# Reworked beginning of a one-core hybrid encoder layer: order of the input, the first weights and the first products

## Chip, core and metric

The kernel runs on one core of one Trainium2 chip. The metric is the device time of one execution in microseconds, as the median of several runs. The core has five engines: PE (TensorE, matrix products), DVE (VectorE), ACT (ScalarE), POOL (GpSimd) and SP (SyncE), which here only issues DMAs. Each engine works through its own instructions in the order of the program and waits on semaphores for the others.

## The reference

One layer on 512 tokens of 1024 channels, in float32: an RMS norm, one input projection to 11272 columns, two token mixers (an mLSTM and a stick-breaking attention) on parts of these columns, two projections back, gates, and an output projection with a residual.

```python
def reference(x, norm_w, w_in, b_in, conv_w, ...):
    h = rmsnorm(x, norm_w)                    # x * rsqrt(mean(x*x) + EPS) * norm_w
    proj = einsum('bsd,de->bse', h, w_in) + b_in
    (mq, mk, mv, mi, mf, mo, mz, sq, sk, sv, sz, gates) = split(proj, ...)
    ...                                       # mLSTM -> y_m, stick-breaking attention of
    ...                                       # rmsnorm(sq), rmsnorm(sk), sv -> y_s
    merged = g_m * (y_m @ w_proj_m) + g_s * (y_s @ w_proj_s)
    return x + merged @ w_out
```

The change touches only the norm and the first group of columns of the projection: the first 512 of `sq`, the queries of four attention heads.

## The kernel before

Every large product is made of three: each float32 operand is split into a high part (a rounded copy, type fp32r, made by ACT) and a low part (the operand less its high part), and high x high, low x high and high x low are summed in PSUM. The high and low parts of the normed, transposed input are called `hh` and `hl`, eight slices of 128 channels (index k) by 512 tokens; those of the first weights are `fh` and `fl`, eight tiles of 128x512 (index k), kept in the list `f_w`.

The work is a list of units, `units`, each with 512 KB of weights (`stg` is the tile that its DMA fills). In the loop over units, number c issues the evacuation of unit c - 1, the splits of units up to c + 2, then its own products in two halves, `mm(0)` and `mm(1)`, with other work (transposes, attention heads) put between the halves and behind them. The order that is written is the order on each engine. The first four units are special (`first=True` in `tok_group`): their weights are four pieces of 256 rows for the same 512 columns, and their products go by blocks of 128 tokens: unit tb computes block tb with all eight k, 24 products, into its own PSUM bank `f_ps[tb]`. From unit 4 on the general code runs (`mm3`, L85 to L87).

Before the loop stand the DMAs, all issued by SP in this order: the first token block of the input in two halves (`load_x(0)`, L193), the vector `norm_w` (8 rows of `v_rows`, L201), the weights of units 0 and 1 (L109), token block 1, the weights of units 2 and 3, token blocks 2 and 3, and a list of small vectors (`gst`, `load_vecs`). The bias row of the first group (`brow`, L297) and the weights of unit 4 follow from inside the loop.

Then PE gets nine products of a zero tile (`warm`, L910), the transposition of `norm_w` into `nw_t` (`norm_vec`), two further zero products, and the first token block's eight transposes. A token block is prepared in two steps. `x_scale(tb)` lets ACT square it and sum the squares (L271, L274), POOL form the reciprocal root (L260, L261) and DVE scale the block in place (L276). `x_turn(tb)` transposes it on PE in two groups of four (L286); DVE then makes `hh` of each group in one operation (L288) and `hl` in four (L292). The split of the first weights (`first_split`, L890 and L891) has ACT make `fh` and DVE (units 0 and 2) or POOL (units 1 and 3) make `fl`:

```python
    first_split(0)
    x_turn(0)
    first_split(1, nc.gpsimd)
    x_scale(1)
    first_split(2)
    first_split(3, nc.gpsimd)
```

The products of a block go k by k, three for each k (L932 to L934). Between the halves of unit 0 stands `x_turn(1)`, followed by `x_scale(2)`, `x_scale(3)` and POOL's `gates_fill`; between the halves of unit 1 stands `x_turn(2)`, behind them `x_turn(3)`. The evacuation of block 0 (in unit 1's turn, before its products) adds the bias row on DVE (`qraw`, L328) and takes four squares with sums on ACT (`sqj`, L337). Before unit 3's products PE transposes the small vectors (`turn_vecs`, L236 and L237).

Of the kernel before, what the change touches and what calls it, by code (L numbers as in the profile page):

```python
# [16 lines left out]
KT = 8  # L17
# [17 lines left out]
def tile_hybrid_layer(  # L35
# [58 lines left out]
    class Unit:  # L94
# [12 lines left out]
        def load(self, tag="stg"):  # L107
            self.st = blk(tag, shape=self.shape)
            nc.sync.dma_start(self.st, self.ap)  # L109
# [93 lines left out]
    rows(v_rows, 0, norm_w, 8)  # L203
# [59 lines left out]
    def x_scale(tb):  # L263
        xs = tiny.tile([128, 4], F32, name="xs", bufs=2)
        ssq, r = xs[:, 0:2], xs[:, 2:3]
        xn = x_t[tb]
        junk = blk("om", BF, (D,), name="junk")
        if tb == 0:
            for i in range(2):
                c = slice(i * D // 2, (i + 1) * D // 2)  # L270
                nc.scalar.activation(junk[:, c], xn[:, c], AF.Square, accum_out=ssq[:, i:i + 1])  # L271
            nc.gpsimd.tensor_tensor(ssq[:, 0:1], ssq[:, 0:1], ssq[:, 1:2], op=OP.add)
        else:
            nc.scalar.activation(junk, xn, AF.Square, accum_out=ssq[:, 0:1])  # L274
        rstd(r, ssq[:, 0:1], D, EPS)
        nc.vector.tensor_scalar(xn, xn, r, None, op0=OP.mult)  # L276

    def x_turn(tb):
        ts = slice(tb * 128, (tb + 1) * 128)
        xn = x_t[tb]  # L280
        for g in range(2):
            ks = slice(4 * g, 4 * g + 4)
            tp = att_ps()
            for j in range(4):
                kt = g * 4 + j
                nc.tensor.transpose(tp[:, j * 128:(j + 1) * 128], xn[:, kt * 128:(kt + 1) * 128], ident)  # L286
            dh = hh[:, ks, ts]
            nc.vector.tensor_tensor(dh, tp.rearrange("p (k t) -> p k t", k=4),  # L288
                                    nw_t[:, ks].unsqueeze(2).to_broadcast([128, 4, 128]), op=OP.mult)
            for j in range(4):  # L290
                k = 4 * g + j
                nc.vector.scalar_tensor_tensor(hl[:, k, ts], tp[:, j * 128:(j + 1) * 128], nw_t[:, k:k + 1],  # L292
                                               hh[:, k, ts].bitcast(F32), op0=OP.mult, op1=OP.subtract)
# [592 lines left out]
    def first_split(i, low=None):  # L886
        u = units[i]
        for j in range(2):
            hi, lo = blk("qk", FR, name="fh"), blk("y", FR, name="fl")
            nc.scalar.activation(hi, u.st[:, j, :], AF.Copy)  # L890
            (low or nc.vector).tensor_tensor(lo, u.st[:, j, :], hi.bitcast(F32), op=OP.subtract)  # L891
            f_w.append((hi, lo))

# [20 lines left out]
    x_scale(0)  # L914
    warm(2)
    first_split(0)
    x_turn(0)
    first_split(1, nc.gpsimd)
    x_scale(1)
    first_split(2)  # L920
    first_split(3, nc.gpsimd)

    f_ps = []

    def first_mm(tb):
        def mm(half):
            if half == 0:
# [117 lines left out]
```

## Time and profile before

| | |
|---|---|
| median of 3 runs | 719.08 us (718.85 to 719.39) |
| the profiled execution, its own time | 720.13 us |
| its span, first to last instruction | 718.4 us |
| mean granted clock of PE | 0.997 of full speed |
| PE busy | 709.8 us, 3356 products and transposes |
| DVE / ACT / POOL busy | 424.5 / 315.8 / 93.5 us |
| HBM read / written | 65.12 / 2.10 MB |

Times in the trace run from the start of the span. Lines are lines of the kernel; a name such as `dps<-fh,hh` is output and inputs. An entry "idle before" with an arrow is the idle time of the engine ahead of an instruction and what ended it. The end of a product on PE is modelled, since products are pipelined, so the distance between two starts says more than a duration.

### The profile page before, as it was taken

Reading aid. Unit: us, or ns where it says so; the run is one execution under the profiler, and the core shown is the slowest. Engines: PE = TensorE matmul, PEld = TensorE weight load, DVE = VectorE, ACT = ScalarE, POOL = GpSimd, SP = SyncE. Lnnn points to the kernel's source line nnn. Section 1 sums busy time; section 2 is a strip of 40 time slices with the busy share of each in tenths; the row PEclk is TensorE's granted clock in tenths of the full one; section 3 lists DMA queues with packets and bytes.
Section 4 is the critical chain, followed back from the end, with each engine's and each line's share of the span. In section 5 each row is a group of like instructions: output and inputs, shape, how many; then the busy total and the mean of one; then the engine's idle time right before and its main releaser. Section 6 shows DMA issues by size and latency. Waiting matters only on the chain.

```text
span 718.4 us, 9058 instructions
## 1 busy us (share of the span) xinstructions
PE 709.8 (99%) x3356; PEld 593.1 (83%) x3356; DVE 424.5 (59%) x663; ACT 315.8 (44%) x601; POOL 93.5 (13%) x235
## 2 busy tenths in 40 slices
PE   7999999999999999999999999999999999999997
PEld 5888888888888888888888888888888888888886
DVE  5837886656487568279944737994343254556441
ACT  5245364476255544244475534447554343222210
POOL 5422022253022112000001110000112000000000
PEclk9999999999999999999999999999999999999999
DMA  6433332233323222333332233333223333333621
GB/s 239 133 103 81 109 86 77 69 95 92 99 62 87 58 86 62 102 91 97 101 94 59 63 99 88 91 100 89 74 59 89 89 91 97 104 88 89 234 89 58
DMA packets 91475, 67.80 MB, mean 94 GB/s; under 512 B 3470, under 2 KB 77608, under 8 KB 91432
## 3 DMA queue, kind: packets, MB, share of 16 engines
q1 hardware_dynamic: 91432, 67.23, 32.8%
q8 instruction: 26, 0.43, 0.2%
q14 instruction: 17, 0.14, 0.1%
HBM read 65.12 MB, written 2.10 MB: 94 GB/s over the span
## 4 chain that ended last, share of the span: by engine, by line
PE 97%; DMA 1%; DVE 1%; POOL 0%; SPq 0%; issue 0%; ACT 0%; DVEq 0%
PE dps L85 28%; PE dps L87 27%; PE dps L86 27%; PE aps L86 2%; PE aps L87 2%; PE aps L85 2%; PE aps L440 1%; PE aps L382 1%; DMA stg<-in_w_in_dram 1%; PE dps L934 1%; PE dps L932 1%; PE dps L933 1%; PE aps L735 1%; PE aps L736 1%; PE aps L737 1%; DVE fl L891 0%
## 5 line engine op out<-in xcount | busy, mean ns | idle before, releaser
L91 DVE TENSOR_TENSOR wl<-stg,wh 128x1024 fp32r<-128x1024 f32 x108 | 132.3, 1225 | 140.3 <-ACT wh L90 139.9
L85 PE MATMUL dps<-hh,wh 128*128 128x512 f32 x448 | 175.8, 392 | 0.0
L86 PE MATMUL dps<-hl,wh 128*128 128x512 f32 x448 | 174.6, 390 | 0.0
L87 PE MATMUL dps<-hh,wl 128*128 128x512 f32 x448 | 174.6, 390 | 0.0
L90 ACT ACTIVATE wh<-stg 128x1024 fp32r<-128x1024 f32 x108 | 113.6, 1052 | 95.3 <-PE dps L87 58.6
L87 PEld LDWEIGHTS dps<-hh,wl 128*128 128x128 f32 x448 | 84.1, 188 | 17.7
L85 PEld LDWEIGHTS dps<-hh,wh 128*128 128x128 f32 x448 | 84.2, 188 | 17.5 <-issue 1.0
L86 PEld LDWEIGHTS dps<-hl,wh 128*128 128x128 f32 x448 | 84.2, 188 | 16.6
L85 PE MATMUL dps<-wh,hh 128*128 128x512 f32 x224 | 88.3, 394 | 0.0
L87 PE MATMUL dps<-wh,hl 128*128 128x512 f32 x224 | 87.4, 390 | 0.0
L86 PE MATMUL dps<-wl,hh 128*128 128x512 f32 x224 | 87.4, 390 | 0.0
L87 PEld LDWEIGHTS dps<-wh,hl 128*128 128x128 f32 x224 | 42.1, 188 | 8.9
L86 PEld LDWEIGHTS dps<-wl,hh 128*128 128x128 f32 x224 | 42.1, 188 | 8.2
L85 PEld LDWEIGHTS dps<-wh,hh 128*128 128x128 f32 x224 | 42.1, 188 | 8.2
L626 DVE SCALAR_TENSOR_TENSOR acc<-tmp,vec,acc 128x511 f32<-128x511 f32 (+2 forms) x48 | 36.0, 750 | 1.7
L629 ACT ACTIVATE tmp<-acc 128x512 f32<-128x512 f32 x16 | 10.1, 633 | 50.2 <-DVE acc L626 50.2
L415 DVE TENSOR_TENSOR_SCAN om<-om 128x512 f32<-128x512 f32 (+3 forms) x32 | 27.9, 871 | 6.3 <-POOL om L409 6.3
L409 POOL TENSOR_SCALAR_AFFINE_SELECT om<-om 128x128 f32<-128x128 f32 x32 | 12.1, 378 | 134.5 <-ACT om L407 134.5
L90 ACT ACTIVATE at_split<-aps 128x384 fp32r<-128x384 f32 (+1 forms) x24 | 11.8, 525 | 36.8 <-PE aps L440 36.8
L688 POOL TENSOR_SCALAR_AFFINE_SELECT w_all<-om 128x128 f32<-128x128 f32 x16 | 4.1, 293 | 168.9 <-DVE om L683 168.9
L91 DVE TENSOR_TENSOR at_split<-aps,at_split 128x384 fp32r<-128x384 f32 (+1 forms) x24 | 13.7, 599 | 19.8 <-ACT at_split L90 19.8
L86 PE MATMUL dps<-wl,mgh 128*128 128x512 f32 x64 | 24.9, 389 | 0.0
(239 smaller groups left out, 1170.6 us busy)
## 6 DMA issues: line engine op xcount, KB each, us to landing
stg<-in_w_in_dram SPq DMA_DIRECT2D x87, 512.0 KB, 3.7
stg<-in_w_proj_s_dram SPq DMA_DIRECT2D x8, 512.0 KB, 3.7
stg<-in_w_proj_m_dram SPq DMA_DIRECT2D x8, 512.0 KB, 3.6
stg<-in_w_out_dram SPq DMA_DIRECT2D x8, 512.0 KB, 3.7
brow<-in_b_in_dram SPq DMA_DIRECT2D x8, 256.0 KB, 4.2
xr<-in_x_dram SPq DMA_DIRECT2D x8, 256.0 KB, 5.7
out_dram<-xr SPq DMA_DIRECT2D x7, 256.0 KB, 2.3
x<-in_x_dram SPq DMA_DIRECT2D x3, 512.0 KB
```

The source lines that it names most:

```text
L85: nc.tensor.matmul(ps, ah, bh, start=first, stop=False)
L86: nc.tensor.matmul(ps, ah, bl, start=False, stop=False)
L87: nc.tensor.matmul(ps, al, bh, start=False, stop=last)
L90: nc.scalar.activation(hi, src, AF.Copy)
L91: nc.vector.tensor_tensor(lo, src, hi.bitcast(F32), op=OP.subtract)
L382: nc.tensor.transpose(tp[:, tb * 128:(tb + 1) * 128], self.raw[name][tb][:, hs], ident)
L409: nc.gpsimd.affine_select(out=om[:, ts], in_=om[:, ts], compare_op=OP.is_gt, fill=1.0, base=0, channel_multiplier=1, pattern=[[-1, 128]])
L415: nc.vector.tensor_tensor_scan(back, back, back, 1.0, op0=OP.mult, op1=OP.bypass)
L440: nc.tensor.transpose(tp[:, at + (i - j) * 128:at + (i - j + 1) * 128], a_t[i][:, j * 128:(j + 1) * 128], ident)
L626: nc.vector.scalar_tensor_tensor(acc[:, j:], t[:, 0:T - j], cw(3 - j, ch), acc[:, j:], op0=OP.mult, op1=OP.add)
L629: nc.scalar.activation(t, acc, AF.Sigmoid)
L735: nc.tensor.matmul(nm[:, 0:258], ph, vh, start=j == 0, stop=False)
```

## The change

- The DMA of `norm_w` is issued by ACT and no longer by SP. (`Unit.load` gets a parameter `by` for the issuing engine that no call uses.)
- `x_scale` is cut in two: `x_square` (ACT; the factor 1/D is put into the squares) and `x_scale` (POOL and DVE). For block 0 POOL needs one operation less, and DVE scales it in two halves.
- `x_turn`: block 0's `hh` are made by DVE as before, those of blocks 1 to 3 by ACT, one copy for each k. The `hl` come as functions that the caller places.
- `first_split` is cut into `first_high` (ACT) and `first_low` (always DVE). ACT's order stays: `fh` of units 0 and 1, the square of block 1, `fh` of units 2 and 3. On DVE block 0's `hh` and `hl` come first, then the scaling of block 1, four `fl`, block 1's `hl`, the other four `fl`, the scalings of blocks 2 and 3.
- Products: `first_a` issues the two products with `fh` (all `hh` of its k, then all `hl`), `first_b` the one with `fl`. Block 0 begins with its 16 products of `first_a`; then, behind block 1's transposes, come four of `first_b`, the 16 of block 1's `first_a`, and block 0's last four. Unit 1's turn has block 1's eight products of `first_b`, four on either side of block 2's transposes. Blocks 2 and 3 have `first_a` and `first_b` by halves.
- Warm-up: 9, 3 and 2 zero products instead of 9 and 2; the last two stand behind block 0's transposes.

```diff
--- before.py
+++ after.py
@@ -104,9 +104,9 @@
             self.slow = None
             self.heavy = False
 
-        def load(self, tag="stg"):
+        def load(self, tag="stg", by=None):
             self.st = blk(tag, shape=self.shape)
-            nc.sync.dma_start(self.st, self.ap)
+            (by or nc.sync).dma_start(self.st, self.ap)
 
         def split(self):
             self.wh = blk("wh", FR, self.shape)
@@ -200,7 +200,7 @@
     def rows(dst, lo, src, n):
         nc.sync.dma_start(dst[lo:lo + n, :], src.rearrange("(r p) -> r p", p=128))
 
-    rows(v_rows, 0, norm_w, 8)
+    nc.scalar.dma_start(v_rows[0:8, :], norm_w.rearrange("(r p) -> r p", p=128))
     ident = cst.tile([128, 128], F32, name="ident")
     make_identity(nc, ident)
     mhalf = cst.tile([128, 8], F32, name="mhalf")
@@ -260,37 +260,51 @@
         nc.gpsimd.tensor_scalar(dst, ssq, 1.0 / n, eps, op0=OP.mult, op1=OP.add)
         nc.gpsimd.tensor_tensor(dst, dst, mhalf[:, 0:dst.shape[1]], op=OP.pow)
 
-    def x_scale(tb):
+    def x_square(tb):
         xs = tiny.tile([128, 4], F32, name="xs", bufs=2)
-        ssq, r = xs[:, 0:2], xs[:, 2:3]
         xn = x_t[tb]
         junk = blk("om", BF, (D,), name="junk")
-        if tb == 0:
-            for i in range(2):
-                c = slice(i * D // 2, (i + 1) * D // 2)
-                nc.scalar.activation(junk[:, c], xn[:, c], AF.Square, accum_out=ssq[:, i:i + 1])
-            nc.gpsimd.tensor_tensor(ssq[:, 0:1], ssq[:, 0:1], ssq[:, 1:2], op=OP.add)
-        else:
-            nc.scalar.activation(junk, xn, AF.Square, accum_out=ssq[:, 0:1])
-        rstd(r, ssq[:, 0:1], D, EPS)
-        nc.vector.tensor_scalar(xn, xn, r, None, op0=OP.mult)
+        n = 2 if tb == 0 else 1
+        for i in range(n):
+            c = slice(i * D // n, (i + 1) * D // n)
+            nc.scalar.activation(junk[:, c], xn[:, c], AF.Square, scale=D ** -0.5, accum_out=xs[:, i:i + 1])
+        return xs
+
+    def x_scale(tb, xs):
+        xn = x_t[tb]
+        r = xs[:, 2:3]
+        n = 2 if tb == 0 else 1
+        nc.gpsimd.tensor_scalar(r, xs[:, 0:1], xs[:, 1:2] if tb == 0 else 0.0, EPS, op0=OP.add, op1=OP.add)
+        nc.gpsimd.tensor_tensor(r, r, mhalf[:, 0:1], op=OP.pow)
+        for i in range(n):
+            c = slice(i * D // n, (i + 1) * D // n)
+            nc.vector.tensor_scalar(xn[:, c], xn[:, c], r, None, op0=OP.mult)
 
     def x_turn(tb):
         ts = slice(tb * 128, (tb + 1) * 128)
         xn = x_t[tb]
+        low = []
         for g in range(2):
             ks = slice(4 * g, 4 * g + 4)
             tp = att_ps()
             for j in range(4):
                 kt = g * 4 + j
                 nc.tensor.transpose(tp[:, j * 128:(j + 1) * 128], xn[:, kt * 128:(kt + 1) * 128], ident)
-            dh = hh[:, ks, ts]
-            nc.vector.tensor_tensor(dh, tp.rearrange("p (k t) -> p k t", k=4),
-                                    nw_t[:, ks].unsqueeze(2).to_broadcast([128, 4, 128]), op=OP.mult)
-            for j in range(4):
-                k = 4 * g + j
-                nc.vector.scalar_tensor_tensor(hl[:, k, ts], tp[:, j * 128:(j + 1) * 128], nw_t[:, k:k + 1],
-                                               hh[:, k, ts].bitcast(F32), op0=OP.mult, op1=OP.subtract)
+            if tb == 0:
+                nc.vector.tensor_tensor(hh[:, ks, ts], tp.rearrange("p (k t) -> p k t", k=4),
+                                        nw_t[:, ks].unsqueeze(2).to_broadcast([128, 4, 128]), op=OP.mult)
+            else:
+                for j in range(4):
+                    k = 4 * g + j
+                    nc.scalar.activation(hh[:, k, ts], tp[:, j * 128:(j + 1) * 128], AF.Copy, scale=nw_t[:, k:k + 1])
+
+            def lows(g=g, tp=tp):
+                for j in range(4):
+                    k = 4 * g + j
+                    nc.vector.scalar_tensor_tensor(hl[:, k, ts], tp[:, j * 128:(j + 1) * 128], nw_t[:, k:k + 1],
+                                                   hh[:, k, ts].bitcast(F32), op0=OP.mult, op1=OP.subtract)
+            low.append(lows)
+        return low
 
     def bias_row(c0):
         b = blk("brow")
@@ -883,13 +897,15 @@
 
     f_w = []
 
-    def first_split(i, low=None):
-        u = units[i]
+    def first_high(i):
         for j in range(2):
             hi, lo = blk("qk", FR, name="fh"), blk("y", FR, name="fl")
-            nc.scalar.activation(hi, u.st[:, j, :], AF.Copy)
-            (low or nc.vector).tensor_tensor(lo, u.st[:, j, :], hi.bitcast(F32), op=OP.subtract)
+            nc.scalar.activation(hi, units[i].st[:, j, :], AF.Copy)
             f_w.append((hi, lo))
+
+    def first_low(k):
+        hi, lo = f_w[k]
+        nc.vector.tensor_tensor(lo, units[k // 2].st[:, k % 2, :], hi.bitcast(F32), op=OP.subtract)
 
     units[0].load()
     units[1].load()
@@ -911,27 +927,55 @@
 
     warm(9)
     norm_vec()
-    x_scale(0)
+    xs0 = x_square(0)
+    warm(3)
+    x_scale(0, xs0)
+    first_high(0)
+    first_high(1)
+    low0 = x_turn(0)
     warm(2)
-    first_split(0)
-    x_turn(0)
-    first_split(1, nc.gpsimd)
-    x_scale(1)
-    first_split(2)
-    first_split(3, nc.gpsimd)
-
-    f_ps = []
+    low0[0]()
+    xs1 = x_square(1)
+    first_high(2)
+    first_high(3)
+    low0[1]()
+    x_scale(1, xs1)
+    for k in range(4):
+        first_low(k)
+
+    f_ps = [None] * TB
+
+    def first_a(tb, ks):
+        if 0 in ks:
+            f_ps[tb] = dense_ps()
+        for p in range(2):
+            for k in ks:
+                nc.tensor.matmul(f_ps[tb], h_sta(k, tb)[p], f_w[k][0], start=p == 0 and k == 0, stop=False)
+
+    def first_b(tb, ks):
+        for k in ks:
+            nc.tensor.matmul(f_ps[tb], h_sta(k, tb)[0], f_w[k][1], start=False, stop=k == KT - 1)
+
+    lo_k, hi_k = range(4), range(4, 8)
 
     def first_mm(tb):
         def mm(half):
-            if half == 0:
-                f_ps.append(dense_ps())
-            for k in range(4 * half, 4 * half + 4):
-                sh, sl = h_sta(k, tb)
-                wh, wl = f_w[k]
-                nc.tensor.matmul(f_ps[tb], sh, wh, start=k == 0, stop=False)
-                nc.tensor.matmul(f_ps[tb], sl, wh, start=False, stop=False)
-                nc.tensor.matmul(f_ps[tb], sh, wl, start=False, stop=k == KT - 1)
+            if tb == 0 and half == 0:
+                first_a(0, lo_k)
+                first_a(0, hi_k)
+            elif tb == 0:
+                first_b(0, lo_k)
+                first_a(1, lo_k)
+                first_a(1, hi_k)
+                first_b(0, hi_k)
+            elif tb == 1 and half == 0:
+                first_b(1, lo_k)
+            elif tb == 1:
+                first_b(1, hi_k)
+            else:
+                ks = hi_k if half else lo_k
+                first_a(tb, ks)
+                first_b(tb, ks)
         return mm
 
     for tb in range(TB):
@@ -992,10 +1036,14 @@
         ahead(c)
         units[c].mm(0)
         if c < 2:
-            x_turn(c + 1)
+            low = x_turn(c + 1)
+            low[0]()
+            low[1]()
         if c == 0:
-            x_scale(2)
-            x_scale(3)
+            for k in hi_k:
+                first_low(k)
+            for tb in (2, 3):
+                x_scale(tb, x_square(tb))
             gates_fill()
         for g in list(act):
             if c in REST:
@@ -1010,7 +1058,8 @@
                 act.append(g)
         units[c].mm(1)
         if c == 1:
-            x_turn(3)
+            for fn in x_turn(3):
+                fn()
     now[0] = N
     units[N - 1].evac()
     assert not act and not pend and not later, (act, pend, later)
```

## Rows read from the trace of the kernel before

**Rows 1.** The profile's page: busy time, share of the span, instructions; and the chain's shares.

```profile
PE 709.8 (99%) x3356; PEld 593.1 (83%) x3356; DVE 424.5 (59%) x663; ACT 315.8 (44%) x601; POOL 93.5 (13%) x235
...
PE 97%; DMA 1%; DVE 1%; POOL 0%; SPq 0%; issue 0%; ACT 0%; DVEq 0%
```

**Rows 2.** Timeline of PE: start, duration, engine, line, operation, count, idle before.

```profile
1.50 4.21 PE L910 MATMUL dps<-idle 128*128 128x512 f32 x9 [1.50 <-DVE idle L905]
...
10.66 0.64 PE L932 MATMUL dps<-fh,hh 128*128 128x512 f32 x1 [2.43 <-DVE hh L288]
...
14.39 0.40 PE L932 MATMUL dps<-fh,hh 128*128 128x512 f32 x1
...
14.86 0.39 PE L934 MATMUL dps<-fl,hh 128*128 128x512 f32 x1
...
15.88 0.48 PE L932 MATMUL dps<-fh,hh 128*128 128x512 f32 x1
...
17.68 0.50 PE L934 MATMUL dps<-fl,hh 128*128 128x512 f32 x1 [0.41 <-DVE fl L891]
...
26.53 0.48 PE L932 MATMUL dps<-fh,hh 128*128 128x512 f32 x1
...
32.07 0.25 PE L236 MATMUL aps<-ident,v_rows 98*128 98x98 f32 x1
```

**Rows 3.** Windows: stretch, length, busy time by engine, granted clock, DMA share, GB/s.

```profile
10.60:11.00 0.40, 0.34 (x1) 0.23 (x2) 0.40 (x2) 0.40 (x1) 0.40 (x1) 0.74 1.10 435
...
14.00:14.50 0.50, 0.50 (x3) 0.36 (x3) 0.50 (x2) 0.26 (x2) 0.50 (x1) 0.80 0.24 55
14.50:15.00 0.50, 0.50 (x4) 0.41 (x3) 0.50 (x1) 0.50 (x1) 0.50 (x1) 1.00 0.17 47
```

**Rows 4.** Timeline of ACT.

```profile
7.96 1.15 ACT L890 ACTIVATE fh<-stg 128x512 fp32r<-128x512 f32 x2 [3.12 <-DMA stg<-in_w_in_dram]
9.29 1.15 ACT L890 ACTIVATE fh<-stg 128x512 fp32r<-128x512 f32 x2 [0.19 <-DMA stg<-in_w_in_dram]
10.53 1.06 ACT L274 ACTIVATE junk<-x 128x1024 bf16<-128x1024 f32 x1
...
13.05 1.15 ACT L890 ACTIVATE fh<-P 128x512 fp32r<-128x512 f32 x2
...
23.95 0.31 ACT L337 ACTIVATE sqj<-qraw 128x128 bf16<-128x128 f32 x1 [7.14 <-DVE qraw L328]
...
25.56 1.04 ACT L90 ACTIVATE wh<-stg 128x1024 fp32r<-128x1024 f32 x1
```

**Rows 5.** Timeline of SP's DMA issues.

```profile
1.68 0.36 SPq L201 DMA_DIRECT2D v_rows<-in_norm_w_dram  x1
...
18.18 0.35 SPq L297 DMA_DIRECT2D brow<-in_b_in_dram  x1
```

**Rows 6.** Windows (columns as in rows 3): the DMA's rate as the weights begin.

```profile
2.50:3.00 0.50, 0.50 (x3) 0.38 (x2) 0.00 (x0) 0.00 (x0) 0.00 (x0) 1.00 1.04 397
...
3.50:4.00 0.50, 0.50 (x3) 0.40 (x2) 0.00 (x0) 0.50 (x1) 0.00 (x0) 1.00 0.88 112
```

**Rows 7.** Timeline of DVE.

```profile
8.62 1.29 DVE L891 TENSOR_TENSOR fl<-stg,fh 128x512 fp32r<-128x512 f32 x2 [1.72 <-ACT fh L890]
...
10.55 1.13 DVE L292 SCALAR_TENSOR_TENSOR hl<-aps,nw_t,hh 128x128 fp32r<-128x128 f32 x4
...
13.47 0.75 DVE L276 TENSOR_SCALAR x<-x,xs 128x1024 f32<-128x1024 f32 x1
14.14 3.49 DVE L891 TENSOR_TENSOR fl<-stg,fh 128x512 fp32r<-128x512 f32 x2
...
23.22 0.69 DVE L328 TENSOR_TENSOR qraw<-dps,brow 128x512 f32<-128x512 f32 x1 [0.36 <-PE aps L286]
```

**Rows 8.** Timeline of POOL.

```profile
10.00 2.51 POOL L891 TENSOR_TENSOR fl<-stg,fh 128x512 fp32r<-128x512 f32 x2 [3.96 <-ACT fh L890]
```

**Rows 9.** ACT's groups by line and shape: copies or sigmoids of one PSUM block.

```profile
L411 ACT ACTIVATE a_all<-aps,rq 128x128 f32<-128x128 f32 x8 | 3.0, 377 | 0.0
```

## Prediction

> **What bounds the kernel now.** The page comes first: PE is busy for 99% of the span and the chain that ended last is 97% PE [rows 1]. So a change at the beginning is worth only what it takes out of PE's order of work before PE runs without a gap. PE's timeline shows where that is [rows 2]: warm-up products from 1.50, the first real product at 10.66 after 2.43 us of idling, one more wait of 0.41 us before 17.68, and then no gap. I measure everything at one point, called E: the transposes of the small vectors at 32.07, which follow the third block's products. Before E lie 72 products and three sets of eight transposes in both kernels, and after E the program is unchanged. A block of 24 products takes 32.07 - 26.53 = 5.54 us, 0.231 us each; a set of transposes costs 15.88 - 14.86 - 0.23 = 0.79 us.
>
> Three things made E late. The first product waited for the weights' first part and for DVE, which made low parts of weights before the input's operands [rows 7]. The granted clock fell from 2.4 to 1.2 GHz at about 10.8, after the 2.43 us pause, and came back by 14.3, after PE had worked without a pause [rows 2, 3]: nine products took 14.39 - 10.66 = 3.73 us, not 9 x 0.231 = 2.08. And a low part made by DVE came late, because a pair took 3.49 us where another had taken 1.29 [rows 7]; during it POOL was making low parts too, of which it needs 2.51 us a pair [rows 8]. Last, ACT's timeline gives the pace: a pair of high parts at 7.96, at 9.29, a square, two further pairs, the last at 13.05 [rows 4]. Its first two pairs waited for DMAs, and from there it never rests.
>
> **The change part by part.** *DMAs.* The vector norm_w leaves SP's queue, where it took 0.36 us [rows 5], and goes to ACT's, where it is issued before ACT has data to work on; the weights and everything behind them on SP are issued 0.36 us earlier. ACT's whole chain hangs on the first weights, so I move it by 0.36 us. Below: nothing, if the transfers are limited by what is under way and not by when they are issued. Above: in the half microsecond after 3.5 the rate was 112 GB/s where it had been 397 [rows 6]; if the small vector caused that, 0.5 x (1 - 112/397) = 0.36 us more, 0.72 in all. I take 0.36, as only that row names this DMA. The Trainium skill (DMA: Bandwidth & Descriptors, Issuing engines are not separate DMA queues) says that a DMA started by another engine runs on the same 16 DMA engines and saves only issuing time; by that the shift is 0.36 us and not 0.72. No row of before has a DMA on a second queue, so the trace does not test it.
>
> *Input.* One POOL operation less, two half scalings in place of one, more warm-up products, and DVE free for the first block's operands: the first product comes up from 10.66 to about 9. That alone is worth nothing, as the products behind it now wait one by one for ACT's high parts, in the same order on ACT as before.
>
> *Order of the products.* The first block now needs only high parts of weights for its first 16 products, and transposes of the second block follow. When ACT's last high part is ready, at 13.05 + 1.15 - 0.36 = 13.84, eleven products are done (eight of the first half, three of the second) and 61 are left before E, with three sets of transposes. If PE then runs freely at 2.4 GHz, E comes at 13.84 + 61 x 0.231 + 3 x 0.79 = 30.30, a gain of 1.77 us, and the third block could start at 30.30 - 5.54 = 24.76.
>
> *Low parts of the weights.* All eight are now DVE's, in order behind the second block's scaling; POOL makes none, so I take the undisturbed 1.29 us a pair [rows 7]. DVE's whole list from the second scaling is 0.75 + 4 x 1.29 + 2 x 1.13 + 2 x 0.75 = 9.67 us. The scaling began at 13.47 behind POOL's low parts, which are gone; it can begin between about 12.2 and 13.1, so DVE is through between 21.9 and 22.8. On the way, the fourth low part is ready between 15.5 and 16.4 (needed at 13.84 + 5 x 0.231 + 0.79 + 3 x 0.231 = 16.5) and the eighth, 1.5 us before the end, between 20.4 and 21.3 (needed 20 products after the fourth, at 21.1). PE needs the third block's scaled input five products later, at 22.3. These parts cost nothing as long as nothing else holds DVE; if it comes later, the first block's last product is late by as much.
>
> *High parts of the input on ACT.* For blocks two to four they move from DVE to ACT, eight copies a block in place of two DVE operations. For the second block ACT is idle by then. For the third they are queued behind the first block's evacuation: the bias addition on DVE at 23.22, then four squares with their sums on ACT from 23.95 to 25.56 [rows 4, 7]. Before, that had no reader in a hurry. The bias addition had waited 0.36 us, and the releaser named is PE; but the first block's products had ended at 17.68 + 6 x 0.231 = 19.1, so it was the bias row's DMA, issued at 18.18 [rows 5]. It too is behind SP's list, so it moves by 0.36 us. Hence: addition at 22.86, squares from 22.86 + 0.73, through at + 1.61, and the first copy done after 0.38 us, the duration of an ACT operation on one 128x128 block of PSUM [rows 9]: 25.58. PE is ready at 24.76 and now waits 0.82 us, a wait that takes the place of the one removed. Behind the waiting product stands everything PE has left. The copies then pace the first four products: no loss if one follows another in 0.231 us, 3 x 0.146 = 0.44 us if each takes its full 0.377; I take 0.2, halfway. E = 25.58 + 5.54 + 0.2 = 31.32.
>
> *Sum.* 32.07 - 31.32 = 0.75 us. The profiled execution took 720.13 us (span 718.4, 1.73 us around it); its like would take 719.4 with a span of 717.65. Against the median of the runs, 719.08, the forecast is 718.3.
>
> **The rivals.** *The DMAs do not move.* Then the copy is done at 25.94, E is 31.68 and the gain 0.39: 718.7. For it: at 10.6 the DMA engines moved 435 GB/s with a share above 1 and had no room [rows 3]; against: ACT's first pair waited 3.12 us for a DMA whose issue moves [rows 4].
>
> *The evacuation does not hold the third block.* If the bias row lands earlier and DVE is through at 21.9, the copies are ready when PE is, and E is 30.3 to 30.5: gain 1.6 to 1.8, 717.4; with the 0.36 us of the low rate as well, 717.0. For it: DVE's list may be shorter than its sum, since neighbours overlap. Against: the row's DMA is behind the same list on SP as before.
>
> *The clock falls later, and the kernel becomes slower.* From 9 to 14 us PE works in single products with pauses between, as ACT delivers. One pause of 2.43 us brought the clock down, the one of 0.41 us before 17.68 did not [rows 2]. If it falls when the dense work starts, at about 14, one stretch like that of before costs 1.65 us; the third block can start at 26.41, the wait for the copies disappears in it, E is 31.95 and the time 719.0. The gain is gone when the loss passes 26.53 - 24.76 = 1.77 us; a second stretch of the same kind, after the next pause, costs 1.65 us more: 720.6, slower than before. The Trainium skill (TensorE: Matmul & The Clock Gate, A second HAM failure mode: psum-queue depth-cycling) tells of a kernel in which short pauses between groups of products made the clock swing between its levels, which speaks for this rival; the one short pause in this trace speaks against it.
>
> **How the numbers follow.** Forecast case 0.45; DMAs unmoved 0.10; evacuation not in the way 0.25; clock down for one stretch 0.13, for two 0.07. A measurement of this kernel tells from no change about 0.2%, 1.44 us. Faster by more than that is the second rival and a tail of 0.02 of the forecast case: 0.27. Slower is the second stretch: 0.07. The rest, 0.66, is within 0.2%. The range goes from 717.0, the lowest of the second rival, to 719.6, between one stretch and two, and leaves out a little under 0.2: the two stretches and sums of several gains. The forecast case alone spans 717.8 to 718.9 (shift 0 to 0.72 us, pacing 0 to 0.44).
>
> **What would show it right or wrong.** The first pair of high parts on ACT should start 0.36 us earlier, at about 7.6, and the last end at about 13.84. PE's first product should start near 9, and the clock should read 2.4 GHz after 14. POOL should have no low parts, and DVE's pairs 1.29 us. Before the third block PE should wait for an ACT copy, by 0.8 us, with the first block's squares just before that copy on ACT. The transposes of the small vectors should start at 31.3. The prediction is wrong if ACT's chain starts elsewhere, if the granted clock is low after 14, if DVE's list ends after 23 or if the bias row lands before 22.

## The result, and the profile after

The changed kernel takes 721.22 us (median of 8 runs, 720.41 to 721.98), the kernel before 719.03 in the same set (718.65 to 719.39): a ratio of 1.003, 95% interval 1.0019 to 1.0041. It is slower by 0.3%. The forecast was 718.3 with a range of 717.0 to 719.6; the measured time is outside it, on the other side of 719. The profiled execution of the changed kernel is the slowest of its 8 runs, 721.98 us with a span of 720.0. (The code counts blocks from 0: its blocks 2 and 3 are the third and the fourth.)

The page looks as before [rows 1]: PE busy for 99%, and the chain that ended last is PE.

```profile
PE 712.6 (99%) x3359; PEld 593.5 (82%) x3359; DVE 421.1 (58%) x662; ACT 322.2 (45%) x625; POOL 89.2 (12%) x230
...
PE 96%; DMA 1%; ACT 1%; POOL 0%; SPq 0%; issue 0%; DVE 0%; DVEq 0%; ACTq 0%
```

PE's timeline (start, duration, operation, idle before):

```profile
8.73 1.70 PE L953 MATMUL dps<-fh,hh 128*128 128x512 f32 x4
...
13.39 1.24 PE L953 MATMUL dps<-fh,hh 128*128 128x512 f32 x2 [0.32 <-ACT fh L903]
14.43 1.91 PE L953 MATMUL dps<-fh,hl 128*128 128x512 f32 x4
16.14 1.68 PE L292 MATMUL aps<-ident,x 128*128 128x128 f32 x8
17.57 1.18 PE L957 MATMUL dps<-fl,hh 128*128 128x512 f32 x4
...
22.23 2.23 PE L957 MATMUL dps<-fl,hh 128*128 128x512 f32 x8
...
26.11 1.03 PE L292 MATMUL aps<-ident,x 128*128 128x128 f32 x8
28.14 1.28 PE L953 MATMUL dps<-fh,hh 128*128 128x512 f32 x4 [0.99 <-ACT hh L299]
29.30 1.27 PE L953 MATMUL dps<-fh,hl 128*128 128x512 f32 x4
...
34.06 0.25 PE L236 MATMUL aps<-ident,v_rows 98*128 98x98 f32 x1
```

Beside [rows 2]: the first product comes at 8.73 and not at 10.66, and yet point E, the transposes of the small vectors, comes at 34.06 and not at 32.07. Three places matter. First, from 14.43 PE is slow: the eight transposes of the second block take 1.43 us from start to next start (16.14 to 17.57), not 0.79. Second, the third block's first product, at 28.14, waits 0.99 us for a copy on ACT. Third, its first four products take 1.16 us from start to start (28.14 to 29.30) where four at 0.231 take 0.92. The windows show the first (last columns: granted clock, DMA share, GB/s):

```profile
13.00:14.00 1.00, 0.66 (x3) 0.27 (x2) 1.00 (x2) 0.86 (x2) 0.00 (x0) 1.00 1.01 240
14.00:15.00 1.00, 1.00 (x3) 0.81 (x4) 1.00 (x3) 0.00 (x0) 0.00 (x0) 0.51 0.30 62
...
17.00:18.00 1.00, 1.00 (x7) 0.95 (x7) 0.00 (x0) 0.77 (x4) 0.00 (x0) 0.78 0.09 22
18.00:19.00 1.00, 1.00 (x6) 0.83 (x5) 0.59 (x3) 1.00 (x6) 0.00 (x0) 1.00 0.11 39
```

The clock went down to 1.2 GHz at 14.0, after a microsecond in which PE was busy for two thirds, and came back at about 17.4; in [rows 3] it was down from 10.8 to 14.2. The wait for the copy is explained by ACT, DVE, POOL and SP, in this order:

```profile
7.23 1.15 ACT L903 ACTIVATE fh<-stg 128x512 fp32r<-128x512 f32 x2 [2.02 <-DMA stg<-in_w_in_dram]
...
12.71 1.15 ACT L903 ACTIVATE fh<-P 128x512 fp32r<-128x512 f32 x2 [0.19 <-DMA P<-in_w_in_dram]
17.23 2.18 ACT L299 ACTIVATE hh<-aps,nw_t 128x128 fp32r<-128x128 f32 x8 [3.37 <-PE aps L292]
19.25 1.10 ACT L270 ACTIVATE junk<-x 128x1024 bf16<-128x1024 f32 x1
...
26.13 0.31 ACT L351 ACTIVATE sqj<-qraw 128x128 bf16<-128x128 f32 x1 [4.64 <-DVE qraw L342]
...
27.74 4.22 ACT L299 ACTIVATE hh<-aps,nw_t 128x128 fp32r<-128x128 f32 x16
```

```profile
20.48 1.28 DVE L908 TENSOR_TENSOR fl<-stg,fh 128x512 fp32r<-128x512 f32 x2
...
22.89 0.74 DVE L281 TENSOR_SCALAR x<-x,xs 128x1024 f32<-128x1024 f32 x1
24.08 1.41 DVE L281 TENSOR_SCALAR x<-x,xs 128x1024 f32<-128x1024 f32 x1 [0.45 <-POOL xs L278]
25.42 0.67 DVE L342 TENSOR_TENSOR qraw<-dps,brow 128x512 f32<-128x512 f32 x1
```

```profile
20.53 0.72 POOL L277 TENSOR_SCALAR xs<-xs 128x1 f32<-128x1 f32 x1 [8.32 <-ACT junk L270]
...
23.14 0.91 POOL L278 TENSOR_TENSOR xs<-xs,mhalf 128x1 f32<-128x1 f32 x1
```

```profile
17.78 0.36 SPq L311 DMA_DIRECT2D brow<-in_b_in_dram  x1
```

ACT's first high part starts at 7.23 and the last pair ends at 13.86; forecast were 7.6 and 13.84 [rows 4]. Then ACT waits 3.37 us for the second block's transposes, copies eight slices (2.18 us), and only then, at 19.25, squares blocks 2 and 3, which it had done from 14.44 on before. POOL's roots for them follow at 20.53 to 24.05, next to DVE's low parts, and POOL's operations on one column take 0.72 to 0.91 us. DVE scales the fourth block at 24.08, after a wait for POOL, and that scaling takes 1.41 us where the one ahead of it took 0.74. Behind it on DVE stands the first block's bias addition: 25.42, not 23.22 [rows 7]. The four squares and then the copies follow it on ACT, and the copies of the third block begin at 27.74. The bias row was issued at 17.78 (18.18 before, [rows 5]); DVE did not wait for it.

### The profile page after: what moved, and what is told of

Same layout as the page of the kernel before. It is cut to its first block, busy times and chain, and to the rows that moved or that the text cites. A ratio compares the mean times of both kernels' runs of the same rounds, so it can differ in the third digit from the quotient of the medians.

```text
span 720.0 us, 9077 instructions
## 1 busy us (share of the span) xinstructions
PE 712.6 (99%) x3359; PEld 593.5 (82%) x3359; DVE 421.1 (58%) x662; ACT 322.2 (45%) x625; POOL 89.2 (12%) x230
## 4 chain that ended last, share of the span: by engine, by line
PE 96%; DMA 1%; ACT 1%; POOL 0%; SPq 0%; issue 0%; DVE 0%; DVEq 0%; ACTq 0%
PE dps L85 27%; PE dps L86 27%; PE dps L87 27%; PE aps L86 2%; PE aps L87 2%; PE aps L85 2%; PE dps L953 2%; DMA P<-in_w_in_dram 1%; PE aps L454 1%; PE aps L396 1%; PE aps L749 1%; PE aps L750 1%; PE aps L751 1%; PE dps L957 1%; PE aps L776 0%
## 5 line engine op out<-in xcount | busy, mean ns | idle before, releaser
L85 PE MATMUL dps<-yh,wh 128*128 128x512 f32 x64 | 24.9, 389 | 0.0
```

Source lines behind the costliest of these rows:

```text
L85: nc.tensor.matmul(ps, ah, bh, start=first, stop=False)
```

## The experiments

Sixteen executions were profiled: the two from the start, thirteen new kernels, and the kernel before a second time (e8). Ratios are against runs of the kernel before taken in the same set (its medians: 719.03 to 719.33); they are worked out from all runs and are not quotients of the medians. The last four columns are from the profiled execution: "weights" is the start of the first weights' DMA on SP, "high part" that of the first high part on ACT, "last pair" the end of ACT's last pair of high parts, and E the start of the small vectors' transposes. The first profile of the kernel before has 2.08, 7.96, 14.20 and 32.07. E less "last pair" is what PE still needs once the weights are split, whenever they came.

| run | median us (range) | ratio, 95% interval | weights | high part | last pair | E |
|---|---|---|---|---|---|---|
| changed kernel | 721.22 (720.41 to 721.98) | 1.0030, 1.0019 to 1.0041 | 1.69 | 7.23 | 13.86 | 34.06 |
| e1, copies back on DVE | 719.29 (718.54 to 719.90) | 1.0002, 0.9993 to 1.0010 | 1.68 | 7.59 | 13.84 | 31.67 |
| e2, squares one unit later | 718.97 (718.28 to 719.62) | 0.9998, 0.9989 to 1.0007 | 1.69 | 8.17 | 14.74 | 31.91 |
| e3, pauses filled | 721.10 (720.33 to 721.36) | 1.0025, 1.0015 to 1.0035 | 1.68 | 7.98 | 14.25 | 33.16 |
| e4, e1 and e3 | 719.64 (718.78 to 720.28) | 1.0006, 0.9997 to 1.0015 | 1.68 | 6.83 | 13.11 | 31.32 |
| e5, squares of blocks 2, 3 early | 720.18 (719.51 to 720.64) | 1.0012, 1.0002 to 1.0021 | 1.69 | 7.60 | 13.86 | 32.55 |
| e6, norm_w on SP | 720.00 (719.46 to 721.42) | 1.0013, 1.0005 to 1.0022 | 2.08 | 6.18 | 13.04 | 33.48 |
| e7, before with norm_w on ACT | 719.76 (717.26 to 720.66) | 1.0003, 0.9994 to 1.0012 | 1.68 | 8.34 | 14.61 | 32.40 |
| e8, before again | 719.17 (one run) | | 2.11 | 5.94 | 13.20 | 31.12 |
| e10, e2, e5 and e6 | 719.35 (718.80 to 720.29) | 1.0004, 0.9995 to 1.0012 | 2.08 | 6.18 | 13.19 | 31.31 |
| e11, e2 and e6 | 718.29 (717.92 to 719.38) | 0.9990, 0.9981 to 0.9999 | 2.11 | 6.47 | 13.18 | 30.36 |
| e12, norm_w third on SP | 722.70 (721.20 to 723.88) | 1.0046, 1.0033 to 1.0060 | 1.68 | 7.90 | 14.16 | 33.34 |
| e13, ACT's queue, spaced | 721.22 (719.67 to 721.68) | 1.0026, 1.0017 to 1.0036 | 2.04 | 6.08 | 12.65 | 31.92 |
| e14, norm_w first on SP | 721.02 (719.90 to 721.82) | 1.0018, 1.0009 to 1.0027 | 2.11 | 7.93 | 14.66 | 33.91 |
| e15, other vector on ACT's queue | 719.95 (719.37 to 721.54) | 1.0010, 1.0001 to 1.0019 | 2.09 | 6.04 | 13.28 | 32.08 |

**First set: the queue on ACT or the clock.** Theory Q: the loss is the queue in front of the third block's copies. Theory C, the rival of the prediction: it is the clock. e1 undoes the copies on ACT:

```diff
-            if tb == 0:
+            if True:
                 nc.vector.tensor_tensor(hh[:, ks, ts], ...)
```

> One part of the change undone: the high parts of the input's blocks 2 to 4 are made by DVE again, in two operations a block, and no longer by ACT in eight copies. Theory Q (the queue): in the changed kernel the third block's products wait 0.99 us for the first copy and are paced by the copies after it, because the copies stand on ACT behind the first block's squares; without it PE goes from the fourth block's transposes straight on, about 1.7 us earlier: 719.5. Theory C (the clock): the time is lost in the stretch from 14.0 to 17.4 us where the clock is at 1.2 GHz, the wait is only what is left over; the time stays within 0.5 us of 721.2.

Measured 719.29. PE's rows show the wait gone (26.12 follows the fourth block's transposes) and another one in part in its place: the eight products with low parts take 2.93 us from 20.60 to 23.53, not 1.85. DVE now has the high parts in its list as well; and as ACT has no copies, it squares blocks 2 and 3 early, so that POOL's fills stand beside a pair of low parts, which takes 1.95 us and not 1.28.

```profile
20.60 3.10 PE L957 MATMUL dps<-fl,hh 128*128 128x512 f32 x8
23.53 1.04 PE L292 MATMUL aps<-ident,x 128*128 128x128 f32 x8
...
26.12 1.17 PE L953 MATMUL dps<-fh,hh 128*128 128x512 f32 x4
```

```profile
19.07 1.95 DVE L908 TENSOR_TENSOR fl<-stg,fh 128x512 fp32r<-128x512 f32 x2
```

e2 leaves the copies on ACT and moves what stands in front of them: `norm`, which issues the first block's four squares, is held back to the second block's turn.

```diff
-                if tb < 2 or name == "q" and self.s == 0:
+                if name == "q" and self.s == 0 and tb < 2:
+                    held.append(norm)
+                    if tb == 1:
+                        held[0]()
+                        held[1]()
+                elif tb < 2 or name == "q" and self.s == 0:
                     norm()
```

> The first block's four squares are issued one unit later, behind the copies for blocks 3 and 4, which stay on ACT. Theory Q, if it is the squares in front of the copies: the 0.99 us wait before the third block goes, and with it most of the pacing, 1.2 to 1.7 us: 719.5 to 720.0. If it is the copies' own pace (eight of 0.37 us a block), the wait goes but the first four products of the block stay slow: 720.2. Theory C: within 0.5 us of 721.2.

Measured 718.97, 2.25 us less than the changed kernel and less than any case expected. PE's rows and ACT's:

```profile
25.56 1.03 PE L292 MATMUL aps<-ident,x 128*128 128x128 f32 x8
26.35 1.17 PE L959 MATMUL dps<-fh,hh 128*128 128x512 f32 x4
```

```profile
24.39 4.24 ACT L299 ACTIVATE hh<-aps,nw_t 128x128 fp32r<-128x128 f32 x16 [3.45 <-PE aps L292]
```

The copies begin at 24.39, and when PE goes on at 26.35, without a wait, some seven of the 16 are done (4.24 us for all, 0.27 each). So the squares, and the addition that they wait for, were the queue's loss, and the copies' own pace is not a cost once they start early.

e3 and e4 put zero products into the pauses (`FILL` gives their number behind each of the first 16 products; e4 has e1's edit too):

```diff
+    FILL = [[1, 2, 1, 0, 1, 3, 1, 0], [0, 0, 0, 4, 0, 0, 0, 0]]
...
                 nc.tensor.matmul(f_ps[tb], h_sta(k, tb)[p], f_w[k][0], ...)
+                if tb == 0:
+                    warm(FILL[p][k])
```

> Thirteen zero products are put into the pauses between the first block's first 16 products, so that PE has no long pause between 8.7 and 13.9 us; nothing else is changed, and the real products keep their order. Theory C: the clock stays at 2.4 GHz after 14 us, the second block's transposes come about 1.1 us earlier and the products behind them 1.7 us; as everything that leads to the third block's copies hangs on them, about 1.5 us are gained: 719.7. Theory Q alone: PE arrives earlier and waits longer, no change from 721.2. If the zero products themselves are in the way of real ones: 721.5 or more.

> Both: high parts of blocks 2 to 4 on DVE, and the thirteen zero products. If both losses are real and add: 721.2 - 1.7 - 1.5 = 718.0, below the kernel before (719.0). If one of them only hides the other: the better of the two single ones, 719.5.

Measured 721.10 and 719.64: no gain over the changed kernel and over e1. In e3's profile the clock stays at 2.4 GHz, and the third block waits all the same:

```profile
25.19 1.03 PE L292 MATMUL aps<-ident,x 128*128 128x128 f32 x8
27.24 1.28 PE L954 MATMUL dps<-fh,hh 128*128 128x512 f32 x4 [1.02 <-ACT hh L299]
```

Theory C falls as the cause: of the changed kernel's eight runs one has a mean clock of 0.998, the profiled one; the others have 0.999 to 1.0, at 720.4 to 721.6 us. The clock's fall is an event of some executions. In the profiled one it costs something, as E less "last pair" is 20.20 us there and 18.91 in e3; the medians, 721.22 and 721.10, do not show it. The kernel before has such executions too: of its 30 runs in this set seven have a mean clock of 0.996 to 0.998, and they take 719.2 us on average, the others 719.1.

**Second set: what is late, and the DMA.** e5 issues the squares of blocks 2 and 3 earlier:

```diff
     x_scale(1, xs1)
+    xs2 = x_square(2)
+    xs3 = x_square(3)
...
-            for tb in (2, 3):
-                x_scale(tb, x_square(tb))
+            x_scale(2, xs2)
+            x_scale(3, xs3)
```

> The squares of the input's blocks 2 and 3 are issued on ACT directly behind the weights' high parts, where they stood before the change, and not behind the second block's eight copies; all else is as changed. What is late before the third block: if it is the squares of blocks 2 and 3, behind which POOL's roots come at 20 to 23 us while DVE makes low parts (0.72 to 0.92 us an operation), then the fourth block's scaling, then the first block's bias addition at 24.5 to 25.4, then four squares, then the copy, then the roots are ready at about 17, the addition starts at about 23, the copy is done at about 25.7, PE's wait of 1.0 us goes and 0.2 to 0.5 us of pacing stays: 719.6 to 720.0 against 721.2. If the bias row's DMA or DVE's list holds the addition, nothing changes: 721.2.

Measured 720.18, 1.04 us less, just above the 719.6 to 720.0 expected. ACT's rows: the first block's squares start at 24.60 and the copies at 26.22, 1.5 us earlier than in the changed kernel's profile and 0.6 earlier than in e3's, where the clock did not fall.

```profile
24.60 0.31 ACT L351 ACTIVATE sqj<-qraw 128x128 bf16<-128x128 f32 x1 [5.95 <-DVE qraw L342]
...
26.22 4.21 ACT L299 ACTIVATE hh<-aps,nw_t 128x128 fp32r<-128x128 f32 x16
```

So by the medians POOL's late roots are about half of the queue's loss, net of what the early squares cost elsewhere (see e10). The traces show less: from the last pair to E it is 18.69 us here and 18.91 in e3. How the loss divides between the roots and the squares in front of the copies is not shown.

e6 puts norm_w back on SP, and e7 takes it to ACT's queue in the kernel before:

```diff
-    nc.scalar.dma_start(v_rows[0:8, :], norm_w.rearrange("(r p) -> r p", p=128))
+    rows(v_rows, 0, norm_w, 8)
```

> The vector norm_w goes back to SP's queue, between the input and the first weights; all else is as changed. If the forecast's 0.36 us is right: the weights' first high part starts 0.4 us later in the mean, and as everything follows it, the span is 0.3 to 0.4 us longer. If the time outside the span (2.00 us in the changed kernel's runs, 1.73 in those of the kernel before) comes from the second DMA queue, it returns to 1.73. The two cancel to within 0.2 us: 721.2. If the weights do not care: 720.9.

> That one part alone on the kernel before: norm_w is loaded by ACT, nothing else changes. Forecast's term: span 0.36 us shorter, and 0.27 us more outside of the span if the second queue costs that: 719.0 to 719.1 against 719.15. If the DMAs do not move: 719.4. If the low rate after 3.5 us is due to the small vector: 718.7.

e6: 720.00, 1.2 us faster than the changed kernel, against every expectation. ACT's first high part starts at 6.18, though the weights were issued 0.39 us later:

```profile
6.18 1.15 ACT L903 ACTIVATE fh<-stg 128x512 fp32r<-128x512 f32 x2 [1.35 <-DMA stg<-in_w_in_dram]
```

```profile
18.30 2.53 POOL L277 TENSOR_SCALAR xs<-xs 128x1 f32<-128x1 f32 x1 [6.91 <-ACT junk L270]
```

That execution took 721.21 us, though, 1.2 more than e6's median: one of POOL's operations on one column took 2.53 us in it, and E came at 33.48. So this trace shows early weights, but not what they are worth; e15, below, has the same order of loads in an execution at its median.

e7 is inconclusive in time (its runs spread from 717.26 to 720.66), but its high part is the latest of all, 8.34.

> The kernel before, unchanged, for a second profile. The first profiled execution took 720.13 us, 1 us above the median of its runs, with the clock down from 10.8 to 14.2 us. If the clock's fall is the difference, an execution near 719.1 shows no fall or a shorter one, and the small vectors' transposes at about 31.0 and not at 32.07. If not, its first 32 us look as before and the microsecond lies elsewhere.

e8, the kernel before in an execution near its median (719.17 us, span 717.5). PE, ACT, and the windows:

```profile
8.95 0.47 PE L932 MATMUL dps<-fh,hh 128*128 128x512 f32 x1 [0.80 <-ACT fh L890]
...
13.30 1.09 PE L286 MATMUL aps<-ident,x 128*128 128x128 f32 x8 [1.21 <-DVE x L276]
...
16.68 0.50 PE L934 MATMUL dps<-fl,hh 128*128 128x512 f32 x1 [0.73 <-DVE fl L891]
...
31.12 0.25 PE L236 MATMUL aps<-ident,v_rows 98*128 98x98 f32 x1
```

```profile
5.94 1.15 ACT L890 ACTIVATE fh<-stg 128x512 fp32r<-128x512 f32 x2 [0.92 <-DMA stg<-in_w_in_dram]
...
12.05 1.15 ACT L890 ACTIVATE fh<-P 128x512 fp32r<-128x512 f32 x2
```

```profile
11.00:12.00 1.00, 1.00 (x5) 0.53 (x3) 0.72 (x3) 0.91 (x2) 0.83 (x3) 1.00 1.02 418
...
14.00:15.00 1.00, 0.87 (x7) 0.44 (x5) 1.00 (x2) 0.92 (x3) 1.00 (x2) 1.00 0.18 27
```

The weights are there at 5.94 and not at 7.96 [rows 4], the first product starts at 8.95 and not at 10.66 [rows 2], the clock reads 1.00 where it was half [rows 3], and E is 31.12. The microsecond between the first profile and the median lies there. It is no more than the weights moved by: ACT's last pair ends 1.00 us earlier (13.20, not 14.20) and E comes 0.95 earlier. That the first product starts 1.71 us earlier and that the clock stays up gain nothing beyond that, as PE then waits 1.21 us for the second block's scaling and 0.73 for a low part. So E is as early as expected of a clock that stays up, but the weights explain it: E less "last pair" is 17.87 us in the first profile, 17.92 here, and 17.79 in e7, where the clock fell again.

**Third set: do the losses add, and why do the weights land late?** e10 joins e2, e5 and e6; e11 joins e2 and e6.

> The changed kernel with the first block's squares one unit later, the squares of blocks 2 and 3 early, and norm_w on SP's queue. If the queue on ACT (2.2 us) and the second DMA queue (1.2 us) are separate losses that add: 721.2 - 2.2 - 1.2 = 717.8, faster than the kernel before (719.2). If both losses end in the same wait before the third block, undoing the second gains nothing more: 719.0.

> The first block's squares one unit later and norm_w on SP's queue; the squares of blocks 2 and 3 stay behind the second block's copies. Additive: 717.8. If POOL's late roots and the fourth block's late scaling still hold PE once the rest is out of the way, it stays 0.3 to 0.6 us above the run with all three undone: 718.2.

e11 is the best kernel, 718.29, faster than the kernel before by 0.1% (0.9990, 0.9981 to 0.9999). The 718.2 expected was right for a wrong reason: e11 was to lie above e10. e10, with one more edit that had gained by itself, is 1.06 us worse, and its E is 0.95 later with the last pair at the same time. PE's rows of e10 and of e11:

```profile
20.22 3.10 PE L965 MATMUL dps<-fl,hh 128*128 128x512 f32 x8
23.16 1.04 PE L292 MATMUL aps<-ident,x 128*128 128x128 f32 x8
```

```profile
19.98 2.40 PE L963 MATMUL dps<-fl,hh 128*128 128x512 f32 x8
22.21 1.04 PE L292 MATMUL aps<-ident,x 128*128 128x128 f32 x8
...
30.36 0.25 PE L236 MATMUL aps<-ident,v_rows 98*128 98x98 f32 x1
```

With the early squares ACT begins the second block's copies at 15.71 and not at 15.15, DVE's list gets later, one of its pairs of low parts takes 1.70 us and not 1.29 beside POOL's fills, and the eight products with low parts take 2.94 us and not 2.23. What e5 had gained was the way to the third block's copies, and e11 has taken the squares out of that way already.

e12 and e13 were to separate the second queue from the place of the weights. e12 has `rows(v_rows, 0, norm_w, 8)` behind the first two weight DMAs; e13 keeps norm_w on ACT's queue and puts the row of sb_q_norm_w on SP between input and weights.

> The changed kernel with norm_w on SP, but behind the first two weight DMAs: the weights are issued right behind the input, as in the changed kernel, and there is no second queue. If the second queue makes the weights land late: 720.0, as with norm_w ahead of the weights. If it is that the weights start while the input is still coming in: 721.2. If norm_w now lands too late for the first block (it is read at about 5.6 us): the first transposed block waits, and the time is above 721.

> The changed kernel, norm_w on ACT's queue, but another small vector (512 bytes, from SP's list of later) is put on SP between the input and the weights, so that these are issued about as late as before the change. If the second queue makes the weights land late: 721.2. If it is the earlier start of the weights: 720.0.

e12 does not tell: norm_w lands too late, PE waits 1.36 us for it, and the time is 722.70.

```profile
7.07 0.24 PE L216 MATMUL aps<-ident,v_rows 8*128 8x8 f32 x1 [1.36 <-DMA v_rows<-in_norm_w_dram]
```

e13 does not tell either: 721.22 speaks for the queue, but its profiled execution, with an early high part (6.08), is the one fast run of ten (719.67; the others 720.58 to 721.68), and of the others there is no trace. So two cleaner ones: e14 has norm_w as SP's first DMA, ahead of the input; e15 has norm_w between input and weights and the row of sb_q_norm_w on ACT's queue.

> The changed kernel with norm_w on SP as the first DMA of all, ahead of the input: no second queue, and the first weights issued right behind the input, which itself is 0.4 us later. If the second queue costs the 1.2 us: about 720.0, as with norm_w between input and weights, plus nothing for the later input, which has 1 us of slack. If the weights' place right behind the input costs it: about 721.2, with the first high part on ACT after 7 us.

> The changed kernel with norm_w on SP between input and weights, where the time was 720.0, and another small vector (512 bytes, read only 25 us later) on ACT's queue at the start. If a second queue as such costs the 1.2 us: 721.2. If it is the weights' place behind the input: 720.0.

e14: 721.02, high part at 7.93. e15: 719.95, high part at 6.04. ACT's rows of the one and of the other:

```profile
7.93 2.44 ACT L903 ACTIVATE fh<-stg 128x512 fp32r<-128x512 f32 x4 [2.43 <-DMA stg<-in_w_in_dram]
```

```profile
6.04 1.15 ACT L903 ACTIVATE fh<-stg 128x512 fp32r<-128x512 f32 x2 [1.10 <-DMA stg<-in_w_in_dram]
```

A second queue is not needed for the loss (e14), and one with 512 bytes on it costs nothing that shows (e15). What e14 shares with the changed kernel is the weights' place right behind the input. In the nine profiles in which nothing stands between the input's DMAs and the weights', the high part starts at 6.83 to 8.34 and the last pair ends at 13.11 to 14.74; of the seven with a small DMA between, six have 5.94 to 6.47 and 12.65 to 13.28, and the first profile of before has 7.96 and 14.20. How a small DMA in between brings this about was not tried. e13 speaks against the place as the whole cause: it has the DMA between, norm_w on ACT's queue, and the changed kernel's median. Whether norm_w's 4 KB on that queue cost something by themselves, or 512 bytes in between do not suffice, no run separates.

## Why the prediction was wrong

Two steps failed: the size of the queue on ACT, and the sign of the DMA term. E less "last pair" keeps them apart, as it hardly depends on when the weights came (17.79 to 17.92 us in the three profiles with the order of before). The prediction put it at 31.32 - 13.84 = 17.48 us, against 17.87 in its profile of the kernel before. In the five profiles that leave the copies where the change put them and show neither a fall of the clock nor POOL's operation of 2.53 us (e3, e12, e13, e14, e15) it is 18.80 to 19.27. In e2 and e11, without the squares in front of the copies, it is 17.17 and 17.18.

**High parts of the input on ACT**: the mechanism was right, with its place; the size was not. A wait of 0.82 us and 0.2 us of pacing were forecast, 1.02 in all. By E less "last pair" the queue cost 1.6 to 2.1 us; by the medians undoing it gave 2.25 (e2) and 1.93 (e1). The step that failed is "addition at 22.86", held by the bias row. It was held by DVE's list (25.42 in the profiled execution, 24.53 in e3 with the clock up; in e8, too, DVE does not wait before it, at 21.80): I had the scalings of blocks 2 and 3 in that list, but not that their squares now stand behind the copies on ACT, that the roots follow on POOL, and that POOL's operations on one column (0.72 to 0.91 us) and a scaling (1.41) take longer there than the 0.19 to 0.56 and 0.75 that they took in the same work for the first two blocks before. The prediction's own sign of being wrong, DVE's list ending after 23, came true. e5 puts this part at 1.04 us by its median.

**DMAs**: the term of 0.36 us has the wrong sign. The weights were issued 0.39 us earlier, as forecast, but the last pair ended later than in the six executions with a small DMA between and early weights (12.65 to 13.28, against 13.86), and e6 shows 1.2 us for it by its median. The lower end I had given was nothing; a loss had not been bounded. Why the weights come later stays open. That the first high part (7.23) and the last (13.86) stand close to the forecast 7.6 and 13.84 is luck: the forecast was counted from that one of the two profiles of before in which the weights were late. The Trainium skill's rule (DMA: Bandwidth & Descriptors, Issuing engines are not separate DMA queues), that another issuing engine saves only issuing time, agrees with e15, 719.95 us with a vector on ACT's queue against 720.00 in e6 without; it says nothing about what stands in the gap.

**The clock**: the rival came true in the profiled execution, at 14.0 as told, and is not the cause: e3. That the loss would hide in the wait for the copies was wrong too; the way to the copies hangs on the second block's transposes and moved with them.

**Three things made E late**: e8 shows that two of them, the late first product and the clock, had no price of their own, since PE waits for the same chain without them. The sum did not use them. Nor did it harm the sum that its profile was 1.05 us above the median: the last pair and E were late by the same microsecond.

**Input**: the first product was forecast at about 9 and came at 8.73; the kernel before has it at 8.95 in e8. **Low parts of the weights**: POOL makes none, two pairs on DVE take 1.28 us each, as forecast; that they cost nothing is not quite so, as the eight products that need them take 2.23 us in e11 where eight at 0.231 take 1.85. **Order of the products**: from the last pair PE was to need 30.30 - 13.84 = 16.46 us if it ran freely; e2 and e11 need 0.7 more, about half of it for those low parts. That e11's E (30.36) meets the free run's 30.30, and its median (718.29) the forecast of 718.3, is chance: its weights came early, and it has neither the queue nor the moved DMA. The rest of the change is worth about 0.7 us in E less "last pair" and 0.89 by the medians of e11's set (718.29 against 719.18); the queue and the moved DMA took that back and more.

Left open: "after E the program is unchanged" holds for PE, whose last product starts 681.70 us after E in both kernels (at 713.77 and 715.76). But the span less E is 685.9 to 686.0 us in all thirteen kernels of the changed kind and 686.3 to 686.4 in the three profiles of the other kind, and outside of the span the former take 0.10 to 0.27 us more than the kernel before in the same set (the changed kernel's runs: 2.00 us on average, the kernel before 1.73). The latter does not follow the second queue alone: e7 has 1.74 with it, e6 1.88 without.

## What to carry to other kernels

A start that depends on DMA landings can differ by 2 us between executions of one program (the first high part at 5.94 and at 7.96), so two profiles are best compared from the event that PE's order hangs on, here the last high part, and not from the start. Work that is moved to an engine with idle time lands in a queue: what stands in front of it there, and what that in turn waits for on other engines, has to be followed to its end. An earlier DMA issue is a term of its own sign, to be measured, and of two edits that each gain alone, one may only lengthen the other's way (e10).

## What the runs showed of the hardware

- The first high part, which needs the first 512 KB of weights, started at 6.83 to 8.34 us in nine profiles with those weights issued right behind the input (at 1.68 to 1.69, in e14 at 2.11), and at 5.94 to 6.47 in six of seven with a DMA of 4 KB or 512 bytes between (weights issued at 2.04 to 2.11); the seventh has 7.96.
- In the changed kernel's profile POOL's operations on one column took 0.24 to 0.57 us for the first two blocks and 0.72 to 0.91 later, beside DVE's low parts of the weights and a scaling; one of them in e6 took 2.53. A scaling on DVE beside POOL's fills took 1.41 us (changed kernel) or 1.87 (e2) instead of 0.74, and a pair of low parts there 1.70 (e10) or 1.95 (e1) instead of 1.28.
- In the first 20 us the granted clock fell to 1.2 GHz in three of the sixteen profiles: after a pause of PE of 2.43 us in the first profile of before, after one of 2.76 in e7, and in the changed kernel's after pauses of at most 0.69.
